# Loading the b21 slices of a seven-product block during the fifth product instead of the sixth

## The chip, the cores and the metric

The kernel runs on one core of one Trainium2 chip. The metric is the device time of one execution in microseconds (us). The kernel before takes 2382.98 us, the median of three runs (2380.82 to 2383.87).

## What is computed

The reference is a decoder trunk of two layers on 256 tokens of width 2048, in float32. Each layer normalises its input, projects it with one large matrix `w_in`, feeds two token mixers (eight heads of differential attention, sixteen heads of stick-breaking attention), gates each mixer's output, projects both, merges them by two sigmoid gates and adds one last projection to the residual:

```
h = rms_norm(x, norm_gain)
proj = h @ w_in            # da_q da_k da_v da_z sb_q sb_k sb_v sb_z gate_a gate_b, 2048 columns each
ua = rms_norm(differential_attention(...)) * (1 - lambda_init) * silu(da_z)
ub = stick_breaking_attention(...) * silu(sb_z)
y = sigmoid(gate_a) * (ua @ w_branch_a) + sigmoid(gate_b) * (ub @ w_branch_b)
x = x + y @ w_out
```

## The kernel before, in words

**Weights in slices.** Every weight matrix is cut into chunks of 512 columns, and each chunk into eight slices of 256 rows (128 partitions x 1024 float32, 512 KB). A slice is loaded into a tile `raw` by `load_raw` (line 91, the DMA is issued on SyncE's queue at line 93). There are twelve `raw` tiles (`RAW = 12`). `split_raw` (line 96) makes two tiles of it: ScalarE copies it in a rounded form into `wh` (four buffers, line 65), and VectorE writes the remainder into `wl` (three buffers, line 66). When VectorE has written `wl`, nothing reads `raw` any more, and its place is free for another load, unless the block still needs it. Each product of a slice is then three matmuls on TensorE (`mm3`, lines 70 to 72): high times high, high times low, and low times high; they read `wh`, `wh` and `wl`.

**Two kinds of streams.** `c_stream` (line 121) multiplies one chunk in the plain way: eight steps, one slice and 12 matmuls each, summed in PSUM tiles `mc`. `s_stream` (line 149) multiplies two neighbouring chunks at once with seven products instead of eight, each of four steps of one slice and six matmuls, 28 steps in all. It uses four groups of four slices: b11 and b21 (upper and lower half of the left chunk), b12 and b22 (of the right one). In the order of the program, for the variant that the change touches:

- first product, `sU`: the b11 slices are loaded into four tiles `xs`; after each step, GpSimd issues a DMA that adds b12 to `xs[i]` (line 169);
- second product, `sN`: the b22 slices are loaded into four tiles `zs`;
- third product, `sQ`, reads `xs[i]`; then VectorE adds `zs[i]` to `xs[i]` (line 173) and GpSimd issues a DMA that adds b12 to `zs[i]`;
- fourth product, into `sU` again, reads `xs[i]`;
- fifth product, `sQ` (line 235), reads `zs[i]`: each of its steps frees one `zs` tile;
- sixth product, `sN` (line 246), loads the b21 slices into four tiles `ws` and reads them; after each step VectorE adds `ws[i]` to `xs[i]` (`add_w`, line 242, by way of line 173), and `ws[i]` is free;
- seventh product, into `sQ`, reads `xs[i]` and frees it.

The names first to seventh product are used below. The flag `tb_dma` selects a variant in which the b12 and b22 additions are made by DMA and the fifth product comes before the fourth; it is on for the first three stick-breaking groups of each layer and off for the last group and for the three blocks of the merge that compute the gates (`gate_block`, line 855). So each layer has four blocks of the variant above, and the program has eight. In the merge they run beside the plain streams of `w_a` and `w_b`; they are called gate block one, two and three below.

**The order of the work.** `run` (line 256) interleaves two streams: it always takes the next step of the one that is relatively further behind. In the merge 64 units of plain streams (each chunk has eight steps and two empty ones, `GAP`) run beside 84 steps of three blocks. What `run` yields is the order of the program. From this order and from a time model a scheduler at build time derives one fixed order for each engine and for each DMA queue. The splits and the additions of line 173 are under `high_priority(offset=400)` (lines 98, 168, 172): they count as 400 places earlier in the program than they stand. The loads have no such offset. The scheduler gives a load one of the twelve `raw` places when it is free, and the load waits for the last reader of that place.

Around the fifth and sixth product of gate block two, `run` gives this order of slices (worked out from its rule; a3 l4 is the fifth slice of the last chunk of `w_a`, and "five 0" is the first step of the fifth product):

```
five 0, a3 l4, five 1, five 2, a3 l5, five 3, a3 l6, six 0 (ws0), a3 l7, six 1 (ws1), six 2 (ws2), six 3 (ws3)
```

After this come the first slices of `w_b`, and in the first chunk of `w_b` three reloads of a gated mixer output (`reload("b", ...)`, line 763, called at line 838): a `raw` tile is loaded from DRAM and split into tiles `ub`.

Of the kernel before, what the change touches and what calls it, by code (L numbers as in the profile page):

```python
# [42 lines left out]
def trunk(ctx: ExitStack, tc: tile.TileContext, x, xT, norm_gain, w_in, qk_gain, lam_vecs,  # L43
# [24 lines left out]
    def mm3(ps, lh, ll, rh, rl, start, stop, more=False):  # L68
        kw = dict(skip_group_check=True) if more else {}
        nc.tensor.matmul(ps, lhsT=lh, rhs=rh, start=start, stop=False, **kw)  # L70
        nc.tensor.matmul(ps, lhsT=lh, rhs=rl, start=False, stop=False, **kw)  # L71
        nc.tensor.matmul(ps, lhsT=ll, rhs=rh, start=False, stop=stop, **kw)  # L72
# [12 lines left out]
    def raw_tile():  # L85
        return wp.tile([P, KK * CW], F32, name="raw", bufs=RAW)

    def held(nm):
        return wp.tile([P, CW], F32, name="pp", bufs=PPB)

    def load_raw(src):
        raw = raw_tile()
        nc.sync.dma_start(out=raw, in_=src)
        return raw

    def split_raw(raw):
        h = wp.tile([P, KK * CW], F32R, name="wh", bufs=4)
        l = wp.tile([P, KK * CW], F32R, name="wl")
        with tc.high_priority(offset=400):
            split(h, l, raw)  # L100
        return h, l
# [47 lines left out]
    def s_stream(sl, sr, xh, sm, fin, tb_dma=False):  # L149

        hk = KP // 2
        b11, b21, b12, b22 = sl[:hk], sl[hk:], sr[:hk], sr[hk:]
        xs, zs, ws = [None] * hk, [None] * hk, [None] * hk

        def a(half, t):  # L160
            ts = slice(t * P, (t + 1) * P)
            return [xh[i][:, half * KT // 2:(half + 1) * KT // 2, ts] for i in range(2)]

        def s(j):
            return [sm[i][:, j] for i in range(2)]

        def add_dma(dst, src):
            with tc.high_priority(offset=400):
                nc.gpsimd.dma_start(out=dst, in_=src, accum_op=ALU.add)  # L169

        def add(dst, src):
            with tc.high_priority(offset=400):
                nc.vector.tensor_tensor(out=dst, in0=dst, in1=src, op=ALU.add)  # L173

        def prod(ps, lhs, get, after=None, more=False):
            for i in range(hk):
                raw = get(i)
                h, l = split_raw(raw)
                for kk in range(KK):
                    k = i * KK + kk  # L180
                    cs = slice(kk * CW, (kk + 1) * CW)
                    mm3(ps, lhs[0][:, k], lhs[1][:, k], h[:, cs], l[:, cs],
                        k == 0 and not more, k == KT // 2 - 1, more)
                if after is not None:
                    after(i)
                if i < hk - 1:
                    yield

        def loader(store, srcs):
            def get(i):  # L190
                store[i] = load_raw(srcs[i])
                return store[i]
            return get


        u_ps = ps_s.tile([P, CW], F32, name="sU")
        yield from prod(u_ps, a(0, 0), loader(xs, b11), lambda i: add_dma(xs[i], b12[i]))
        p1 = held("p1")
        nc.scalar.copy(p1, u_ps)
        yield  # L200

        n_ps = ps_s.tile([P, CW], F32, name="sN")
        yield from prod(n_ps, s(3), loader(zs, b22),
                        (lambda i: add_dma(zs[i], b12[i])) if tb_dma else None)
        yield


        def next_sums(i):
            if tb_dma:
                add_dma(xs[i], b22[i])  # L210
            else:
                add(xs[i], zs[i])
                add_dma(zs[i], b12[i])

        q_ps = ps_s.tile([P, CW], F32, name="sQ")
        yield from prod(q_ps, s(0), lambda i: xs[i], next_sums)
        p5 = held("p5")
        nc.scalar.copy(p5, q_ps)
        yield
        if tb_dma:  # L220
            v_ps = ps_s.tile([P, CW], F32, name="sQ")
            yield from prod(v_ps, s(2), lambda i: zs[i], None, False)
            yield

        yield from prod(u_ps, s(1), lambda i: xs[i], None, True)
        w = held("w")
        nc.vector.tensor_tensor(out=w, in0=u_ps, in1=p5, op=ALU.subtract)
        u = held("u")
        nc.scalar.copy(u, u_ps)
        fin(1, 0, lambda dst: nc.vector.tensor_tensor(out=dst, in0=n_ps, in1=w, op=ALU.subtract))  # L230
        yield

        if not tb_dma:
            v_ps = ps_s.tile([P, CW], F32, name="sQ")
            yield from prod(v_ps, s(2), lambda i: zs[i], None, False)
        fin(1, 1, lambda dst: nc.vector.scalar_tensor_tensor(
            out=dst, in0=v_ps, scalar=-1.0, in1=w, op0=ALU.mult, op1=ALU.subtract))
        if not tb_dma:
            yield


        def add_w(i):
            add(xs[i], ws[i])

        r_ps = ps_s.tile([P, CW], F32, name="sN")
        yield from prod(r_ps, a(1, 0), loader(ws, b21), add_w)
        fin(0, 0, lambda dst: nc.vector.tensor_tensor(out=dst, in0=r_ps, in1=p1, op=ALU.add))
        yield

        yield from prod(v_ps, a(1, 1), lambda i: xs[i], None, True)  # L250
        fin(0, 1, lambda dst: nc.vector.tensor_tensor(out=dst, in0=v_ps, in1=u, op=ALU.add))
        yield
# [159 lines left out]
    for l in range(DEPTH):  # L412
# [37 lines left out]
        def w_chunk(base, g):  # L450
            return [w_in[l, base + g, kp] for kp in range(KP)]
# [324 lines left out]
        for g in range(NG):  # L776
            wT = sb_weights(g)
            if g == NG - 1:
                reload("a", (0, 1), ua)
            v = v_tiles()  # L780
            gz = att.tile([P, NT, CW], F32, name="gz")
            gzT = []

            def z_T():
                gzT.append(att.tile([P, HPG, S], F32, name="gzT", tag="hold"))
                for t in range(NT):
                    tr = ps_at.tile([P, CW], F32, name="at")
                    for h in range(HPG):
                        nc.tensor.transpose(out=tr[:, h * P:(h + 1) * P],
                                            in_=gz[:, t, h * P:(h + 1) * P], identity=ident)  # L790
                    nc.scalar.copy(gzT[0][:, :, t * P:(t + 1) * P], heads(tr))

            fv, fz = vz_fin(v, gz, z_T)
            s = s_stream(w_chunk(SB_V, g), w_chunk(SB_Z, g), xt, sm,
                         lambda col, t, op: (fv, fz)[col](t, op), g + 1 < NG)
            if g + 1 < NG:
                c = [q_stream(NG + g + 1, xt, False, GAP), k_stream(NG + g + 1, xt, False, GAP)]
            else:
                c = [gate_chunk("a", 0), gate_chunk("a", 1)]
            run((len(c) * (C_STEPS + GAP), chain(*c)), (S_STEPS, s))  # L800
            last_u = sb_out(g, wT, v, gzT[0])
# [53 lines left out]
        def gate_block(b, c):  # L855
            return s_stream(w_chunk(GATE_A if b == "a" else GATE_B, c),
                            w_chunk(GATE_A if b == "a" else GATE_B, c + 1), xt, sm, sig_s_fin(b, c))
# [98 lines left out]
```

## Time and profile before

| What | Value |
|---|---|
| Median of three runs | 2382.98 us (2380.82 to 2383.87) |
| The profiled execution, its own time | 2380.12 us |
| The profiled execution, span from the first to the last instruction | 2378.4 us |
| Bytes moved | 535.55 MB, 225 GB/s over the span |

Times in the profile are counted from the span's start. PE is TensorE, DVE is VectorE, ACT is ScalarE, POOL is GpSimd, SP is SyncE; a q behind the name is the engine's queue, which issues DMAs. A row of the timeline gives start, duration, engine, line, operation, output and inputs, and in brackets the idle time of the engine before it and what ended that idle time. Instructions of the same kind that follow without a gap are merged into one row ("x2").

### The profile page before, as it was taken

To read this page: it belongs to the slowest core of one execution; us is meant where nothing else is said; L and a number is where in the kernel's file an instruction comes from. 1 tells how busy PE (TensorE), PEld (TensorE's weight loads), DVE (VectorE), ACT (ScalarE), POOL (GpSimd) and SP (SyncE) were. 2 spreads that over 40 slices of the span, in tenths; PEclk is the share of its full clock that TensorE was granted. 3 is DMA by queue.
4 is the path that set the end of the run, shared out by engine and by line. 5 is a ranking of instruction groups with operands and counts; after the bars stand their busy time and mean duration, and the time that the engine had idled before them with its cause. 6 is when DMAs were issued, how large, how long until landed. Compare 5 with 4: busy or idle time off the path is not lost.

```text
span 2378.4 us, 31466 instructions
## 1 busy us (share of the span) xinstructions
PE 2356.9 (99%) x10996; PEld 1955.5 (82%) x10996; DVE 1781.6 (75%) x2000; ACT 1529.9 (64%) x2201; POOL 341.1 (14%) x399
## 2 busy tenths in 40 slices
PE   9999999999999999999999999999999999999999
PEld 7888888888888888788888888888888888887887
DVE  6777768688788888786566777676887887878854
ACT  7666666677777666554465666666767776656643
POOL 1231220201101011100020312202011010111000
PEclk9999999999999999999999999999999999999999
DMA  9546546878877888898665465468789778988972
GB/s 367 179 143 210 196 142 221 198 224 235 238 234 209 266 274 247 293 287 271 207 211 177 142 213 187 141 226 209 224 233 241 234 210 254 289 237 285 298 264 89
DMA packets 152239, 535.55 MB, mean 225 GB/s; under 512 B 17360, under 2 KB 17872, under 8 KB 152080
## 3 DMA queue, kind: packets, MB, share of 16 engines
q1 hardware_dynamic: 123552, 432.72, 53.3%
q0 software_dynamic: 28096, 100.42, 19.9%
q8 instruction: 86, 1.41, 0.2%
q14 instruction: 73, 0.60, 0.1%
q10 hardware_dynamic: 432, 0.40, 0.1%
HBM read 509.35 MB, written 24.12 MB: 224 GB/s over the span
## 4 chain that ended last, share of the span: by engine, by line
PE 96%; DMA 2%; DVE 1%; ACT 1%; issue 0%; DVEq 0%; SPq 0%; ACTq 0%
PE mc L71 16%; PE mc L72 16%; PE mc L70 16%; PE sU L71 6%; PE sU L72 5%; PE sU L70 5%; PE sN L71 5%; PE sN L72 5%; PE sN L70 5%; PE sQ L71 3%; PE sQ L70 3%; PE sQ L72 3%; PE at L277 2%; PE at L71 1%; PE at L72 1%; PE at L70 1%
## 5 line engine op out<-in xcount | busy, mean ns | idle before, releaser
L66 DVE TENSOR_TENSOR wl<-raw,wh 128x1024 fp32r<-128x1024 f32 (+1 forms) x1001 | 1212.5, 1222 | 391.9 <-PE mc L71 155.9
L65 ACT CAST wh<-raw 128x1024 fp32r<-128x1024 f32 (+1 forms) x1001 | 1047.5, 1051 | 642.2 <-PE mc L72 340.7
L169 POOL DMA_DIRECT2D raw<-in_w_in x136 | 117.8, 867 | 835.4 <-DVE wl L66 429.3
L71 PE MATMUL mc<-wl,xTh 128*128 128x512 f32 x576 | 225.1, 391 | 2.5 <-DVE wl L66 2.4
L72 PE MATMUL mc<-wh,xTl 128*128 128x512 f32 x576 | 224.4, 390 | 0.0
L70 PE MATMUL mc<-wh,xTh 128*128 128x512 f32 x576 | 206.8, 391 | 0.0
L70 PE MATMUL mc<-wh,xrh 128*128 128x512 f32 x512 | 197.6, 393 | 5.7 <-ACT wh L65 5.7
L71 PE MATMUL mc<-wl,xrh 128*128 128x512 f32 x512 | 200.5, 392 | 0.0
L72 PE MATMUL mc<-wh,xrl 128*128 128x512 f32 x512 | 200.3, 392 | 0.0
L71 PEld LDWEIGHTS mc<-wl,xTh 128*128 128x128 f32 x576 | 108.1, 188 | 26.2 <-DVE wl L66 4.2
L70 PEld LDWEIGHTS mc<-wh,xTh 128*128 128x128 f32 x576 | 107.7, 188 | 22.7 <-ACT wh L65 0.6
L72 PEld LDWEIGHTS mc<-wh,xTl 128*128 128x128 f32 x576 | 108.2, 188 | 21.9
L70 PEld LDWEIGHTS mc<-wh,xrh 128*128 128x128 f32 x512 | 96.6, 189 | 25.5 <-ACT wh L65 5.7
L173 DVE TENSOR_TENSOR raw<-raw 128x1024 f32<-128x1024 f32 x88 | 107.2, 1221 | 13.3 <-DMA raw<-in_w_in 12.2
L71 PEld LDWEIGHTS mc<-wl,xrh 128*128 128x128 f32 x512 | 96.6, 189 | 19.5 <-DVE wl L66 0.2
L72 PEld LDWEIGHTS mc<-wh,xrl 128*128 128x128 f32 x512 | 96.5, 188 | 19.3
L71 PE MATMUL sU<-wl,xrh 128*128 128x512 f32 x256 | 100.7, 393 | 0.1
L72 PE MATMUL sN<-wh,xrl 128*128 128x512 f32 x256 | 100.3, 392 | 0.0
L70 PE MATMUL sN<-wh,xrh 128*128 128x512 f32 x256 | 100.1, 391 | 0.0
L71 PE MATMUL mc<-wl,ua 128*128 128x512 f32 x256 | 100.0, 390 | 0.0
L71 PE MATMUL sN<-wl,xrh 128*128 128x512 f32 x256 | 100.0, 390 | 0.0
L70 PE MATMUL sU<-wh,xrh 128*128 128x512 f32 x256 | 100.0, 390 | 0.0
(254 smaller groups left out, 4913.6 us busy)
## 6 DMA issues: line engine op xcount, KB each, us to landing
raw<-in_w_in SPq DMA_DIRECT2D x583, 512.0 KB, 4.4
raw<-in_w_in POOLq DMA_DIRECT2D x136, 512.0 KB, 7.6
raw<-in_w_a SPq DMA_DIRECT2D x64, 512.0 KB, 5.3
raw<-in_w_b SPq DMA_DIRECT2D x64, 512.0 KB, 5.8
raw<-in_w_o SPq DMA_DIRECT2D x64, 512.0 KB, 4.5
ua<-us POOLq DMA_DIRECT2D x8, 512.0 KB, 5.9
raw<-ua SPq DMA_DIRECT2D x8, 512.0 KB, 4.8
siga<-tok POOLq DMA_DIRECT2D x16, 256.0 KB, 5.3
```

The costliest lines, as they stand in the source:

```text
L65: nc.scalar.copy(h, src)
L66: nc.vector.tensor_tensor(out=l, in0=src, in1=h.bitcast(F32), op=ALU.subtract)
L70: nc.tensor.matmul(ps, lhsT=lh, rhs=rh, start=start, stop=False, **kw)
L71: nc.tensor.matmul(ps, lhsT=lh, rhs=rl, start=False, stop=False, **kw)
L72: nc.tensor.matmul(ps, lhsT=ll, rhs=rh, start=False, stop=stop, **kw)
L169: nc.gpsimd.dma_start(out=dst, in_=src, accum_op=ALU.add)
L173: nc.vector.tensor_tensor(out=dst, in0=dst, in1=src, op=ALU.add)
L277: nc.tensor.transpose(out=tr[:, j * P:(j + 1) * P], in_=src[:, j * P:(j + 1) * P], identity=ident)
```

## The change: what it does

In the variant without `tb_dma`, each step of the fifth product now also issues the load of one b21 slice, after its own matmuls. The sixth product takes the tiles that are there already. The variant with `tb_dma` does what it did before: there `ws[i]` is still empty, and the slice is loaded in the sixth product. No instruction is added or taken away; 32 loads (four in each of eight blocks) stand at another place in the program.

```diff
+        def early(i):
+            ws[i] = load_raw(b21[i])
+
         if not tb_dma:
             v_ps = ps_s.tile([P, CW], F32, name="sQ")
-            yield from prod(v_ps, s(2), lambda i: zs[i], None, False)
+            yield from prod(v_ps, s(2), lambda i: zs[i], early, False)
...
         r_ps = ps_s.tile([P, CW], F32, name="sN")
-        yield from prod(r_ps, a(1, 0), loader(ws, b21), add_w)
+        yield from prod(r_ps, a(1, 0), lambda i: ws[i] if ws[i] is not None else loader(ws, b21)(i),
+                        add_w)
```

With the rule of `run`, the order of slices around the same place of gate block two becomes:

```
five 0 (ws0), a3 l4, five 1 (ws1), five 2 (ws2), a3 l5, five 3 (ws3), a3 l6, six 0, a3 l7, six 1, six 2, six 3
```

## The prediction

> **What bounds the kernel now.** I read the page first, then the busy times by stage, then the list of waits, and then the timelines of the queue and of the engines around the fifth, sixth and seventh product.
>
> ```profile
> span 2378.4 us, 31466 instructions
> PE 2356.9 (99%) x10996; PEld 1955.5 (82%) x10996; DVE 1781.6 (75%) x2000; ACT 1529.9 (64%) x2201; POOL 341.1 (14%) x399
> L65 ACT CAST wh<-raw 128x1024 fp32r<-128x1024 f32 (+1 forms) x1001 | 1047.5, 1051 | 642.2 <-PE mc L72 340.7
> ```
>
> TensorE is busy in all but 21.5 us of the span, and the change takes no matmul away. So only idle time of TensorE can be won, and only where the moved loads have an influence. I asked for the busy times of the eight stretches that begin with the fifth product of a block of the variant without `tb_dma` and end with its seventh. In these rows the columns are the stretch, its length, and the busy time of PE, PEld, DVE, ACT and POOL with the number of instructions, then the granted clock, the busy share of the DMA engines and GB/s; the last row sums all eight.
>
> ```profile
> 940.40:982.00 41.60, 38.41 (x167) 30.90 (x166) 34.99 (x34) 25.18 (x28) 4.74 (x8) 1.00 0.93 325
> 1032.00:1069.10 37.10, 36.72 (x162) 29.72 (x161) 30.58 (x31) 21.73 (x23) 1.68 (x3) 1.00 0.92 318
> ...
> 2125.00:2166.00 41.00, 39.66 (x169) 31.11 (x168) 35.87 (x35) 25.87 (x28) 3.66 (x6) 1.00 0.91 313
> ...
> sum 300.30, PE 295.39 PEld 241.22 DVE 251.64 ACT 189.62 POOL 22.10; mean PE 36.92 PEld 30.15 DVE 31.45 ACT 23.70 POOL 2.76
> ```
>
> The eight stretches hold 300.30 - 295.39 = 4.9 us of idle TensorE. All of it lies in the three stretches shown: 3.2 us and 1.3 us in gate block two of the first and of the second layer, 0.4 us in gate block three of the first. In the other five TensorE never idles. That is all that this change can win if nothing elsewhere moves. For comparison, 0.2% of the kernel, about what a measurement of it can tell from no change, is 4.8 us.
>
> **When the moved loads run now.** The next rows are the queue of SyncE and its waits (in all, times, longest).
>
> ```profile
> SPq L93 <- DVE wl L66: 1812.5, 699, 25.1
> ```
>
> ```profile
> 926.28 8.74 SPq L93 DMA_DIRECT2D raw<-in_w_a  x3
> 937.64 0.33 SPq L93 DMA_DIRECT2D raw<-in_w_in  x1
> 939.90 0.33 SPq L93 DMA_DIRECT2D raw<-in_w_a  x1
> 941.26 0.33 SPq L93 DMA_DIRECT2D raw<-in_w_in  x1
> 941.64 0.90 SPq L815 DMA_DIRECT2D tok<-siga  x2
> 944.73 3.46 SPq L93 DMA_DIRECT2D raw<-in_w_in  x2
> ```
>
> The queue has 699 waits for VectorE to finish reading a `raw` tile: a load goes out when a place is free, not when the program reaches it. The order of issues is that of the program: a3 l4, l5, l6 (the row with x3), ws0, a3 l7, ws1, then ws2 and ws3 (944.73 and, 3.46 - 0.33 later, 947.86). So the b21 slices are already loaded during the fourth and the fifth product; the first matmul of the fifth product comes at about 940.4, where the stretch begins. The words of the change describe the program, not the chip.
>
> From this follows how I treat the edit. Places come free at the same moments as before, since TensorE's pace frees them; the change only permutes which load takes which moment. The eight moments above now go to ws0, a3 l4, ws1, ws2, a3 l5, ws3, a3 l6, a3 l7.
>
> **Part one: the b21 slices come earlier.** ws0 moves from 937.64 to 926.28, ws1 from 941.26 to about 934.7 (the row x3 ends at 926.28 + 8.74 = 935.02, and its last issue took 0.33), ws2 from 944.73 to 937.64, ws3 from 947.86 to 941.26: 6.6 to 11.4 us earlier. Who waits for them today is `add_w` on VectorE. I show this in gate block two of the second layer, by the rows of VectorE, SyncE's queue, ScalarE and TensorE.
>
> ```profile
> DVE raw L173 <- DMA raw<-in_w_in: 12.2, 13, 2.0
> ```
>
> ```profile
> 2135.51 1.22 DVE L173 TENSOR_TENSOR raw<-raw 128x1024 f32<-128x1024 f32 x1 [1.58 <-DMA raw<-in_w_in]
> 2136.66 2.35 DVE L66 TENSOR_TENSOR wl<-raw,wh 128x1024 fp32r<-128x1024 f32 x2
> ```
>
> ```profile
> 2137.90 0.33 SPq L93 DMA_DIRECT2D raw<-ub  x1
> ```
>
> ```profile
> 2142.79 1.05 ACT L65 CAST ub<-raw 128x1024 fp32r<-128x1024 f32 x1 [4.34 <-DMA raw<-ub]
> ```
>
> ```profile
> 2146.29 0.50 PE L71 MATMUL sN<-wl,xTh 128*128 128x512 f32 x1 [0.36 <-DVE wl L66]
> ...
> 2150.63 0.50 PE L71 MATMUL sN<-wl,xTh 128*128 128x512 f32 x1 [0.59 <-DVE wl L66]
> ```
>
> VectorE works in order. It stands 1.58 us for a b21 slice, the two `wl` behind the addition are late, the first of them frees its place only at about 2137.9, the reload of `ub` goes out then, ScalarE stands 4.34 us for it, and with ScalarE late VectorE falls behind until TensorE waits. With the slice there 6 us earlier this wait and the additions (1.22 us each) move into the fourth product, and the reload goes out up to 1.58 + 1.22 = 2.8 us sooner. I take the 1.3 us of this stretch as won. The 0.4 us of gate block three I also take as won, by likeness: a wait of the same kind is among the 13.
>
> In gate block two of the first layer the idle time has two pieces:
>
> ```profile
> 964.57 0.50 PE L71 MATMUL sN<-wl,xTh 128*128 128x512 f32 x1 [0.77 <-DVE wl L66]
> ...
> 976.71 0.50 PE L71 MATMUL sQ<-wl,xTh 128*128 128x512 f32 x1 [2.41 <-DVE wl L66]
> ```
>
> ```profile
> 973.21 1.05 ACT L65 CAST ub<-raw 128x1024 fp32r<-128x1024 f32 x1 [4.39 <-DMA raw<-ub]
> ```
>
> ```profile
> GB/s 242 109 156 359 343 359 351 312 187 320 359 226 226 281 257 281 265 265 312 328 296 257 273 257 320 375 398 437 429 406 421 429 414 406 414 414 398 429 421 437
> ...
> raw<-ub SPq DMA_DIRECT2D x2, 512.0 KB, 7.8
> ```
>
> The first (0.77) is the same backlog, and I take it as won. The second (2.41) hangs on the third reload of `ub`, which lands at 973.2. The last two rows are the transfers of 954 to 975, the rate in 40 slices and the median from issue to landing. Near the end of that stretch the engines move 400 to 437 GB/s, and a load issued a little sooner only queues sooner: I leave the 2.41 us where they are. The Trainium skill ("DMA: Bandwidth & Descriptors", section Bandwidth) puts the ceiling of a core's DMA engines at about 435 GB/s; the last slice, at 437, agrees. By that rule the sum stays as I have it; were the load free to move with its place, the piece would go too and the sum would be 4.9.
>
> Sum of part one: 1.3 + 0.4 + 0.8 = 2.5 us won.
>
> **Part two: the plain stream's slices come later.** a3 l5, l6 and l7 now go out at 939.90, 944.73 and 947.86. When they are needed stands in TensorE's rows: each plain slice opens with a pair of matmuls of line 70, and these are the last three pairs of this chunk, those of l5, l6 and l7.
>
> ```profile
> 948.37 0.61 PE L70 MATMUL mc<-wh,ua 128*128 128x512 f32 x2
> ...
> 952.45 0.61 PE L70 MATMUL mc<-wh,ua 128*128 128x512 f32 x2
> ...
> 956.53 0.61 PE L70 MATMUL mc<-wh,ua 128*128 128x512 f32 x2
> ```
>
> ```profile
> raw<-in_w_a SPq DMA_DIRECT2D x4, 512.0 KB, 4.4
> ```
>
> From issue to first use l5 keeps 8.5 us, l6 7.7 and l7 8.7 (l6 had up to 17.8 before). A landing of 4.4 us, the median from 926 to 951, and the copy to `wh` of 1.05 us need 5.5. So the tightest keeps 2.2 us. Its cost is nothing as long as a landing takes less than 7.7 - 1.05 = 6.65 us; beyond that TensorE stands for the difference.
>
> The tightest place is gate block three, where loads are slower:
>
> ```profile
> raw<-in_w_b SPq DMA_DIRECT2D x5, 512.0 KB, 6.9
> ```
>
> This is the median from 1016 to 1040. With the same 7.7 us it leaves 7.7 - 6.9 - 1.05 = -0.2 us: two such blocks, 0.5 us at most. Since part one empties VectorE's queue at the same place I count this as nothing and keep it for the range.
>
> **Part three: the additions stand elsewhere.** The four additions (4 x 1.22 us) of each block move toward the fourth product. Queued behind each on VectorE are the `wl` of the next slices, for which TensorE waits. In the fourth product of gate block one VectorE is busy 10.68 of 13 us:
>
> ```profile
> 845.00:858.00 13.00, 13.00 (x59) 10.77 (x58) 10.68 (x11) 8.24 (x9) 0.58 (x1) 1.00 0.86 250
> ```
>
> That leaves 2.3 us, so two additions fit there and two stay in the fifth product, from which they came. An addition costs TensorE at most its own 1.22 us where it falls into a dense place, and below nothing it cannot be, as its work is the same. I take nothing, and keep 2 x 1.22 = 2.4 us for the range.
>
> The sum is -2.5 us. Against the profiled execution (2380.12 us, its span of 2378.4 and 1.7 us around it) that is 2377.6; the median of the runs is 2.9 us above that execution, so I forecast 2382.98 - 2.5 = **2380.5 us**.
>
> **The rivals.**
>
> *The additions still chase their loads.* The scheduler puts a prioritised addition where it believes its load has landed, so 13 waits may simply move along with the loads. For it: the loads still go out when a place is free. Against it: the dense stretch of reloads comes after, and would be spared anyway. Then the idle time stays: 2383.0. The Trainium skill ("Trainium Kernel Development and Optimization", Key Constraints) says that DMAs of all queues run on the same 16 engines; the busy shares of 0.91 to 0.93 in the three stretches agree, and speak for this rival.
>
> *Everything goes.* If the third reload does move with its place, all 4.9 us are won: 2378.1.
>
> *The plain stream starves.* Slower: the three late slices have 7.7 us instead of up to 17.8. If landings in these windows take 8.3 us, 1.4 more than the 6.9 measured in gate block three, the tightest slice of each of the six gate blocks is 8.3 + 1.05 - 7.7 = 1.65 us late, together 9.9 us: 2392.9. It begins at 6.65 us. For it: 6.9 stands in a row, and the loads after 954 take 7.8. Against it: the bytes go out at the same moments as before, so the landings should not change.
>
> *It does nothing*, since the loads were early already, falls together with the first rival.
>
> **How the numbers follow.** The forecast gets 0.45, the first rival 0.19, everything goes 0.20, starving 0.16. Faster by over 0.2% means below 2378.2: over half of the third case, and a little of the forecast's, since the order fixed at build time may shift other stalls too; 0.16 in all. How much that can be, the three stretches tell: the same gate block two idles 3.2 us in one layer and 1.3 us in the other, 1.9 us apart. Slower by over 0.2% means above 2387.7: nearly all of the last case, 0.15. The rest, 0.69, lies within. The range goes from 2376.5 (all 4.9 us, and 1.6 us for such a shift) to 2387.5 (no gain, the 2.4 us of part three, the 0.5 us of part two, and 1.6 us); outside it lie most of the starving case and a small remainder below.
>
> **What would show it.** Right: loads of b21 in the queue's rows one to three slices ahead of where they were; no wait of line 173 for a DMA just before the reloads; in gate block two of the second layer the reload goes out 1.5 to 2.8 us sooner relative to its block, and TensorE does not idle there. The 2.41 us before the last `sQ` of the first layer's gate block two remain. Wrong: TensorE idles "<-ACT wh" or "<-DVE wl" at the opening of plain slices during the fifth and sixth product (starving), or the list of line 173's waits has the same sum of about 12 us with the idle time unchanged (chasing), or TensorE's idle time changes in stages that hold none of the eight blocks.

## The result and the profile after

| Kernel | Median | Range | Runs |
|---|---|---|---|
| before | 2381.93 us | 2378.51 to 2383.87 | 6 |
| after | 2392.51 us | 2390.62 to 2395.21 | 6 |

The changed kernel is slower: ratio 1.0049, 95% interval 1.0038 to 1.0060. The forecast was 2380.5 us with a range up to 2387.5; the result lies 5 us above its end. The profiled execution of the kernel after is the slowest of its six, 2395.21 us, 15.1 us above that of the kernel before, while the medians lie 10.6 us apart.

The page of the kernel after:

```profile
span 2393.4 us, 31477 instructions
...
PE 2362.8 (99%) x10996; PEld 1956.7 (82%) x10996; DVE 1781.6 (74%) x2000; ACT 1529.9 (64%) x2201; POOL 341.2 (14%) x399
```

The work is the same: as many instructions on each engine, VectorE busy for the same 1781.6 us. The span has grown by 15.0 us, TensorE's busy time by 5.9, so 9.1 us are new idle time.

Where it lies, by stretches. Each row is one block from its first product to the next block: the stretch, its length, and the busy time of PE, PEld, DVE, ACT and POOL, then the granted clock, DMA share and GB/s. The three rows are gate blocks two and three of the first layer and gate block three of the second; the sum is over all eight blocks that the change touches. First the kernel before:

```profile
891.50:982.00 90.50, 87.31 (x383) 71.42 (x382) 72.91 (x67) 54.44 (x57) 13.32 (x19) 1.00 0.91 279
982.00:1069.00 87.00, 86.62 (x386) 71.01 (x386) 70.03 (x65) 50.98 (x53) 8.26 (x11) 1.00 0.88 272
...
2165.80:2252.10 86.30, 86.30 (x386) 71.11 (x385) 69.97 (x66) 51.02 (x53) 8.26 (x11) 1.00 0.88 273
sum 711.70, PE 703.93 PEld 579.65 DVE 589.39 ACT 456.62 POOL 81.60; mean PE 87.99 PEld 72.46 DVE 73.67 ACT 57.08 POOL 10.20
```

Then the kernel after:

```profile
893.20:989.00 95.80, 89.72 (x384) 72.47 (x383) 73.10 (x67) 54.55 (x57) 13.39 (x19) 0.98 0.87 274
989.00:1078.60 89.60, 87.56 (x386) 70.76 (x385) 69.81 (x66) 50.52 (x53) 8.26 (x11) 1.00 0.83 253
...
2177.20:2267.10 89.90, 87.07 (x386) 70.94 (x385) 69.82 (x66) 50.55 (x53) 8.26 (x11) 1.00 0.84 259
sum 725.80, PE 709.06 PEld 579.83 DVE 589.40 ACT 456.54 POOL 81.60; mean PE 88.63 PEld 72.48 DVE 73.68 ACT 57.07 POOL 10.20
```

The eight blocks are 725.80 - 711.70 = 14.1 us longer, nearly all of the 15.0. They lose 16.74 us of TensorE's time to idling instead of 7.77. Gate block two of the first layer alone grows by 5.3 us, gate block three by 2.6 and 3.6; that of the second layer, where TensorE never idled, now idles 2.8 us.

What the engines wait for, from the lists of waits (in all, times, longest). VectorE in the kernel after, against 12.2 us, 13 times, 2.0 before:

```profile
DVE raw L173 <- DMA raw<-in_w_in: 28.5, 20, 3.5
```

TensorE in the kernel after:

```profile
PE mc L71 <- DVE wl L66: 8.1, 10, 1.5
...
PE sQ L70 <- ACT wh L65: 5.5, 4, 3.8
```

The same two rows in the kernel before:

```profile
PE mc L71 <- DVE wl L66: 2.4, 3, 1.0
...
PE sQ L70 <- ACT wh L65: 0.2, 1, 0.2
```

The waits of `add_w` did not vanish, they more than doubled. How they reach TensorE is seen in gate block three of the first layer of the kernel after. First SyncE's queue: these are the issues of the first, the second and the last of the four b21 slices.

```profile
1022.67 0.33 SPq L93 DMA_DIRECT2D raw<-in_w_in  x1
...
1032.29 0.33 SPq L93 DMA_DIRECT2D raw<-in_w_in  x1
...
1043.11 0.33 SPq L93 DMA_DIRECT2D raw<-in_w_in  x1
```

Then VectorE, in brackets how long it stood before the row:

```profile
1029.90 1.23 DVE L173 TENSOR_TENSOR raw<-raw 128x1024 f32<-128x1024 f32 x1 [2.71 <-DMA raw<-in_w_in]
1031.04 3.49 DVE L66 TENSOR_TENSOR wl<-raw,wh 128x1024 fp32r<-128x1024 f32 x3
1035.60 1.22 DVE L173 TENSOR_TENSOR raw<-raw 128x1024 f32<-128x1024 f32 x1 [1.07 <-DMA raw<-in_w_in]
...
1044.06 1.23 DVE L173 TENSOR_TENSOR raw<-raw 128x1024 f32<-128x1024 f32 x1 [1.37 <-DMA raw<-in_w_in]
...
1051.41 1.23 DVE L173 TENSOR_TENSOR raw<-raw 128x1024 f32<-128x1024 f32 x1 [2.71 <-DMA raw<-in_w_in]
1052.56 2.35 DVE L66 TENSOR_TENSOR wl<-raw,wh 128x1024 fp32r<-128x1024 f32 x2
```

And TensorE:

```profile
1032.31 0.50 PE L71 MATMUL mc<-wl,ub 128*128 128x512 f32 x1 [0.72 <-DVE wl L66]
...
1053.83 0.50 PE L71 MATMUL sQ<-wl,smh 128*128 128x512 f32 x1 [0.70 <-DVE wl L66]
```

The slice goes out at 1022.67, VectorE reaches its addition at 1029.90 - 2.71 = 1027.2 and stands until 1029.9. The `wl` of a `w_b` slice is queued behind the addition, begins at 1031.04, and TensorE goes on at 1032.31, after 0.72 us without work. The same happens at 1051.41, before the pause of 0.70 us that ends at 1053.83. In all four cases VectorE comes to the addition 2.2 to 5.6 us after the issue of the load, and the load lands 3.3 to 8.3 us after it (1035.60 - 1032.29 for the second slice, 1051.41 - 1043.11 for the last).

The largest single loss is in gate block two of the first layer, where the third reload of `ub` now holds up TensorE for longer. ScalarE, and then TensorE:

```profile
977.47 1.04 ACT L65 CAST ub<-raw 128x1024 fp32r<-128x1024 f32 x1 [6.49 <-DMA raw<-ub]
```

```profile
979.51 0.50 PE L70 MATMUL sQ<-wh,xTh 128*128 128x512 f32 x1 [3.81 <-ACT wh L65]
```

Before it was 4.39 us for ScalarE and 2.41 for TensorE. And the pause has an after-effect. In the stretches behind it the column after POOL is the granted clock:

```profile
975.00:979.50 4.50, 0.71 (x4) 0.24 (x2) 0.95 (x1) 2.03 (x3) 0.00 (x0) 1.00 1.03 422
979.50:982.00 2.50, 2.49 (x9) 2.03 (x10) 2.44 (x3) 2.38 (x3) 0.54 (x1) 0.80 1.02 410
982.00:985.00 3.00, 3.00 (x10) 2.34 (x9) 1.51 (x3) 1.04 (x1) 0.00 (x0) 0.60 1.02 408
```

The clock fell to 0.80 and 0.60: 0.2 x 2.5 + 0.4 x 3.0 = 1.7 us of TensorE's speed lost while the page of the profile counts it busy. That is part of the 5.9 us by which busy time grew. The rest was not traced to single rows.

### The profile page after: what moved, and what is told of

It reads as the page before. It is cut to its first block, busy times and chain, and to the rows that moved or that the text cites. A ratio compares the mean times of both kernels' runs of the same rounds, so it can differ in the third digit from the quotient of the medians.

```text
span 2393.4 us, 31477 instructions
## 1 busy us (share of the span) xinstructions
PE 2362.8 (99%) x10996; PEld 1956.7 (82%) x10996; DVE 1781.6 (74%) x2000; ACT 1529.9 (64%) x2201; POOL 341.2 (14%) x399
## 4 chain that ended last, share of the span: by engine, by line
PE 94%; DMA 2%; DVE 2%; ACT 1%; issue 1%; SPq 0%; DVEq 0%; ACTq 0%
PE mc L71 16%; PE mc L72 16%; PE mc L70 16%; PE sU L71 5%; PE sU L70 5%; PE sU L72 5%; PE sN L71 5%; PE sN L72 5%; PE sN L70 5%; PE sQ L70 3%; PE sQ L71 3%; PE sQ L72 3%; PE at L281 2%; DVE wl L66 2%; DMA raw<-in_w_in 1%; PE at L71 1%
## 5 line engine op out<-in xcount | busy, mean ns | idle before, releaser
L173 DVE TENSOR_TENSOR raw<-raw 128x1024 f32<-128x1024 f32 x88 | 107.3, 1222 | 29.3 <-DMA raw<-in_w_in 28.5
```

## The experiments

Theory A: the additions of b21 stand in VectorE's fixed order where the scheduler believes the load to have landed; they move along with the loads, VectorE stands for the loads, and the splits queued behind come late to TensorE. Theory B: the slices of the plain streams, which gave up their turns in the queue, come late.

| Kernel | Median us | Ratio to before (95%) |
|---|---|---|
| after, addition without a load to wait for | 2378.07 | 0.9991 (0.9981 to 1.0000) |
| before, the same | 2375.01 | 0.9975 (0.9966 to 0.9985) |
| after, addition without priority | 2393.58 | 1.0052 (1.0040 to 1.0065) |
| before, the same | 2380.04 | 1.0002 (0.9993 to 1.0011) |
| before, addition behind its split, everywhere | 2395.14 | 1.0063 (1.0050 to 1.0076) |
| after, the same | 2393.17 | 1.0056 (1.0043 to 1.0068) |
| after, loads two steps ahead | 2389.05 | 1.0044 (1.0031 to 1.0058) |
| after, no load to wait for, plain slices ahead | 2377.20 | 0.9986 (0.9977 to 0.9995) |
| after, addition on GpSimd | 2398.59 | 1.0078 (1.0066 to 1.0091) |
| before, the same | 2395.26 | 1.0059 (1.0046 to 1.0071) |
| after, addition behind its split, eight blocks | 2384.26 | 1.0018 (1.0010 to 1.0027) |
| before, the same | 2384.18 | 1.0018 (1.0009 to 1.0027) |
| after, addition by DMA | 2422.90 | 1.0184 (1.0170 to 1.0198) |
| before, the same | 2385.93 | 1.0025 (1.0015 to 1.0034) |
| before, plain slices ahead | 2385.35 | 1.0025 (1.0016 to 1.0034) |
| after, the same | 2390.19 | 1.0044 (1.0031 to 1.0056) |
| after, addition one step early | 2383.32 | 1.0014 (1.0005 to 1.0023) |
| after, addition two steps early | 2378.97 | 0.9996 (0.9988 to 1.0005) |

Each was timed beside the kernel before on the same chip, whose median in the five sets was 2380.59, 2380.89, 2379.71, 2379.80 and 2379.85 us.

**Nothing to wait for.** In both kernels the addition adds the tile `xs[i]` to itself, so that it needs no load; b21 is left out of the seventh product's input. The work of VectorE stays, and so does the order of the loads. But the additions do not stay where they were: with no load to follow, the scheduler puts them earlier. In gate block two of the first layer of the kernel before, the first two moved from 941.75 and 945.47 to 931.29 and 935.83, into the fourth product, which ends at 941.4 there. One row of this run, and one of the kernel before:

```profile
935.83 2.36 DVE L173 TENSOR_TENSOR raw<-raw 128x1024 f32<-128x1024 f32 x2
```

```profile
945.47 1.22 DVE L173 TENSOR_TENSOR raw<-raw 128x1024 f32<-128x1024 f32 x1 [0.77 <-DMA raw<-in_w_in]
```

So the pair takes away the wait and changes the place at once.

```diff
         def add_w(i):
-            add(xs[i], ws[i])
+            add(xs[i], xs[i])
```

> The kernel after, but the addition that follows the sixth product adds xs[i] to itself instead of ws[i]; the b21 slices are therefore left out of the seventh product's input. Same work on VectorE, same loads at the same places, but the addition no longer waits for a load. Theory A (VectorE stands in order for a b21 slice and the wl behind it come late): the loss of 10.6 us goes, 2380 to 2384 us. Theory B (the plain stream's slices come late because the b21 slices hold places, the starving rival of the prediction): the loss stays, 2390 to 2394. Both at work: 2385 to 2389.

> Control: the same edit in the kernel before (xs[i] is added to itself, b21 is left out of the seventh product's input), where 13 waits with 12.2 us in all go. Theory A: a little faster than before, up to the 2 us of TensorE's idle time that hang on these waits, 2379 to 2382. Theory B: no change, 2381 to 2383.

Measured: 2378.07 and 2375.01, both below the range that theory A gave. With no load to wait for, the 10.6 us between the two kernels shrink to 3.1. In the kernel before, the waits and the places of the additions together cost 2380.59 - 2375.01 = 5.6 us. The additions of the two runs stand alike (931.57 and 936.11 in the kernel after), so the 3.1 us that stay come from the order of the loads. They speak for theory B, and ScalarE's waits for plain slices do appear. The kernel after with the self-addition, and below it the kernel before:

```profile
ACT wh L65 <- DMA raw<-in_w_a: 11.6, 9, 3.0
```

```profile
ACT wh L65 <- DMA raw<-in_w_a: 0.4, 2, 0.2
```

**No priority.** The addition loses its offset of 400 places.

```diff
         def add_w(i):
-            add(xs[i], ws[i])
+            nc.vector.tensor_tensor(out=xs[i], in0=xs[i], in1=ws[i], op=ALU.add)
```

> The kernel after with the addition of ws[i] kept, but without its priority of 400 places, so that the scheduler puts it after the splits of its neighbourhood. Theory A: VectorE's waits for b21 slices (28.5 us in the kernel after) fall below 5 us and the loss goes, 2380 to 2385. Theory B: 2390 to 2394.

> Control: the same edit in the kernel before. Theory A: the 12.2 us of waits go, 2379 to 2382; if the late addition instead holds up the seventh product, slower, 2383 to 2390. Theory B: no change, 2381 to 2383.

Measured: 2393.58 and 2380.04, both as without the edit. In the kernel after the waits hardly changed:

```profile
DVE raw L246 <- DMA raw<-in_w_in: 26.6, 17, 3.4
```

So it is not the priority that puts the additions early. The fall in waits that theory A expected here did not come in either kernel (in the kernel before 10.5 us stay of 12.2), so this pair does not tell the theories apart; the scheduler puts an addition early with or without its offset.

**A fixed place behind the split.** Each addition is fixed on VectorE directly behind the split of the same slice in the sixth product. That split reads the slice too, so the addition cannot be the one that stands for the load. First everywhere, and later only in the eight blocks:

```diff
         def add_w(i):
-            add(xs[i], ws[i])
+            if tb_dma:
+                add(xs[i], ws[i])
+            else:
+                tc.keep_in_program_order(nc.vector.tensor_tensor(out=xs[i], in0=xs[i], in1=ws[i], op=ALU.add))
```

> The kernel before, with each addition of a b21 slice fixed on VectorE directly behind the split of that same slice in the sixth product. The split reads the slice, so the addition can no longer be the instruction that stands for the load. Theory A (the additions stand in order for their loads, and the splits queued behind them come late to TensorE): the waits of the addition for a DMA fall from 12.2 us to under 1 us, and the time comes close to the 2375.0 of the kernel before without that wait: 2374.5 to 2377.5. Rival (what costs is not the wait but the place: four additions of 1.22 us between the splits of the sixth product, where VectorE is dense): the waits go too, but the time stays at 2380 or rises above.

> The kernel after, with the same fixed place of the additions. Theory A: the waits of the addition for a DMA fall from 28.5 us to under 1 us and most of the 12 us of loss go. Theory B (the slices of the plain streams come late, since the b21 slices took their turns in the queue) leaves its share: 3 us above the kernel before with the same edit, so 2378 to 2380.5, with 8 to 12 us of waits of ScalarE for slices of w_a. Rival (there is no share B, the 3.1 us between the two kernels without the wait came from another order): the same time as the kernel before with this edit, within 1 us.

> The kernel after with each addition fixed behind the split of its own slice, in the eight changed blocks alone. The earlier run fixed the additions of the six other groups as well, and its stretches show about 2 us lost in each of those, some 11 us in all. Theory A: 2393.2 less these 11 is 2382 to 2384, so that the 12 us of loss are undone apart from what the dense place of the additions costs. Rival (it is the changed blocks that lose in that run): 2390 or more.

> The kernel before with the additions fixed behind the split in the eight blocks alone. By the same reckoning 2395.1 less 12 is 2382 to 2384: without any wait of an addition, the early place that the additions have in the kernel before is worth about as much as their waits cost. Compared with the kernel after under the same edit it shows what the order of the loads does by itself once no addition can stand for a load: theory B says that the kernel after is 2 to 3 us slower, the rival that the two are the same within 1.5 us.

Fixed everywhere, both kernels are slow (2395.14 and 2393.17). Both expectations were missed: the edit also moved the additions of the six `tb_dma` groups, and those cost 2395.14 - 2384.18 = 11 us (9 us in the kernel after). In the eight blocks alone the result is clear: 2384.26 and 2384.18, 0.2 to 0.3 us above what was expected. With the additions at a fixed late place the two orders of the loads take the same time, although the plain slices still come late in the kernel after:

```profile
ACT wh L65 <- DMA raw<-in_w_a: 12.5, 9, 2.8
```

The list of the kernel before has no such row. So late plain slices alone cost nothing that can be measured; theory B fails here. The late place itself costs 4 us in both, though no addition waits for a load in either. A likely reason is that VectorE is dense there (before the edit it is busy 4.94 of the 5 us from 960 to 965, in the sixth product); it was not tried by itself.

**Half the dose.** The kernel after, with each b21 slice loaded two steps ahead of its own step.

```diff
         def early(i):
-            ws[i] = load_raw(b21[i])
+            if i >= 2:
+                ws[i - 2] = load_raw(b21[i - 2])
...
+        def add_and_load(i):
+            add_w(i)
+            if not tb_dma and i < 2:
+                ws[i + 2] = load_raw(b21[i + 2])
```

> Half the dose: in the program each b21 slice is loaded two steps before its own step of the sixth product (two of them in the fifth product, two in the sixth) instead of four or more. Theories A and B both see a smaller permutation: waits of the addition for a DMA between 12.2 and 28.5 us, say 18 to 22, waits of ScalarE for w_a about 4 us, and a time between the two kernels, 2385 to 2389. Rival (a threshold: only the loads in the first two steps of the fifth product meet the rush of other loads): the time of the kernel before, within 2 us.

Measured: 2389.05, between the two kernels, at the upper end of the expected range, with 25.9 us of waits of the addition, more than expected. The rival, which puts it at the time of the kernel before, fails. And ScalarE's list has no wait for `w_a` here, where both theories expected 4 us: so 8 us of loss (1.0044) stand with no late slice of `w_a`.

**Plain slices ahead.** The plain streams of `w_a` and `w_b` load two of their steps ahead, so that they get back about the turns that the b21 slices took.

```diff
         for i, kp in enumerate(depth):
...
-                h, l = split_raw(load_raw(src[kp]))
+                while len(raws) < min(i + 1 + ahead, KP):
+                    raws.append(load_raw(src[depth[len(raws)]]))
+                h, l = split_raw(raws[i])
```

> The kernel after without the addition's wait (each addition adds the tile to itself, so that b21 is left out of the seventh product's input), and besides that the plain streams of w_a and w_b load their slices two of their steps ahead, so that they get back about the turns in the queue that the b21 slices took. Theory B: the waits of ScalarE for slices of w_a fall from 11.6 us to under 4, and of the 3.1 us between 2378.1 (after without the wait) and 2375.0 (before without the wait) at least 2 us go: 2374.5 to 2376.5. Rival (the order of the loads is not the cause, or loading further ahead only delays others in turn): 2378 or above, with the waits merely at another place.

> The kernel before with the slices of w_a and w_b loaded two of their steps ahead in the program, the additions as they are. Theory A: the b21 slices now come later still against the plain ones and the additions are placed behind them; their waits stay near 12 us. In the run of the kernel after with the self-addition gate block two lost its idle time with this edit, the third reload of ub among it; if that holds here, 3 to 5 us go: 2376 to 2379. Rival (what is loaded ahead only takes the turns of others): 2380 to 2384, with waits at other loads.

> The kernel after with the slices of w_a and w_b loaded two of their steps ahead, the additions as they are. If late plain slices carry most of the loss, the time falls from 2392.5 to 2384 or less. If the standing of the additions carries it (theory A), their waits of 28.5 us stay within 5 us and the time stays at 2387 to 2392.

Measured: 2377.20, 2385.35 and 2390.19. Beside the self-addition the edit won 0.9 of the 3.1 us, less than theory B asked for and too little to tell from nothing. ScalarE's waits for `w_a` went altogether, but those for `in_w_in` rose from 21.6 to 29.3 us, as the rival had it. The kernel before lost 5.5 us by the edit, against the expected gain and more than the rival had; why was not traced. The kernel after stayed where it was (1.0044 against 1.0049), and so did the additions' waits, as theory A had it:

```profile
DVE raw L176 <- DMA raw<-in_w_in: 25.1, 19, 3.6
```

**On GpSimd.** The additions of the eight blocks are made by GpSimd.

```diff
-            add(xs[i], ws[i])
+            with tc.high_priority(offset=400):
+                (nc.vector if tb_dma else nc.gpsimd).tensor_tensor(out=xs[i], in0=xs[i], in1=ws[i], op=ALU.add)
```

> The kernel after, with the additions of b21 in the eight blocks that the change touches made by GpSimd instead of VectorE; the computation is the same. GpSimd may stand for the load, and no split is queued behind it. From its rows of 128x256 elements (0.92 to 1.70 us) an addition of 128x1024 should take 3.7 to 6.8 us, four of them up to 27 us, beginning in the fifth product. Theory A (in-order standing of VectorE is what costs): most of the 12 us go, what stays is the share of the late plain slices, 3 us over the kernel before with the same edit; 2378 to 2383. Rival (the early loads themselves cost, through the DMA engines or the reloads of ub): 2388 or more although no addition stands on VectorE.

> The kernel before with the same move of the additions to GpSimd in the eight blocks. Theory A: the 5.6 us that the waits cost go, 2374 to 2377, and VectorE is relieved of 32 additions of 1.22 us besides. Rival (GpSimd's additions are so slow that the splits of the seventh product, which read the sums, come late): above 2383, with TensorE idle for splits at the opening of the seventh product.

Measured: 2398.59 and 2395.26, both slower, and not for a reason that either expectation names. GpSimd in the kernel before with this edit, then VectorE beside it:

```profile
949.32 3.07 POOL L244 TENSOR_TENSOR raw<-raw 128x1024 f32<-128x1024 f32 x1 [3.33 <-DMA raw<-in_w_in]
953.60 6.61 POOL L244 TENSOR_TENSOR raw<-raw 128x1024 f32<-128x1024 f32 x2 [1.21 <-DVE wl L66]
```

```profile
950.20 3.26 DVE L66 TENSOR_TENSOR wl<-raw,wh 128x1024 fp32r<-128x1024 f32 x1
```

```profile
954.53 6.76 DVE L66 TENSOR_TENSOR wl<-raw,wh 128x1024 fp32r<-128x1024 f32 x2
```

These additions take 3.1 to 3.3 us, and a split that begins during one takes 3.3 to 3.4 us instead of 1.22. The first one ends 953.46 - 952.39 = 1.07 us after the addition, so it did nothing until GpSimd had finished. The Trainium skill ("SBUF — State Buffer", Who interferes with whom) says that VectorE and GpSimd share one pair of ports, which one of them holds alone; the trace agrees, with that 1.07. VectorE was still held up, now inside its splits by GpSimd instead of by the load, so this pair tells nothing of theory A.

**By DMA.** In the eight blocks b21 is added to `xs[i]` by an accumulating DMA, which reads it from DRAM once more.

```diff
-            add(xs[i], ws[i])
+            add(xs[i], ws[i]) if tb_dma else add_dma(xs[i], b21[i])
```

> The kernel after, with b21 added to the xs tiles in the eight blocks by an accumulating DMA from DRAM (512 KB each, 32 in all) instead of by VectorE; the computation stays whole. No addition stands on VectorE, and none is queued on GpSimd but the issue of the DMA. Theory A: at least 8 of the 12 us go, 2378 to 2384; the plain slices still come late, by theory B up to 3 us. Rival (the early loads cost by themselves): 2390 or more. A cost on the way could be the 16.8 MB of added traffic, where the DMA engines are over 90% busy: later reloads of ub, some us.

> The kernel before with b21 added by the accumulating DMA in the eight blocks. Theory A: the waits of 12.2 us and 32 additions of 1.22 us leave VectorE, 2374 to 2378, unless the added 16.8 MB delay the reloads of ub. Rival (the added traffic costs more than the waits): above 2382, with longer waits of ScalarE for raw<-ub than 15.0 us. The difference between this run and the kernel after with the same edit is what the order of the loads does with VectorE free of additions: by theory B about 3 us, by the runs with fixed additions about 0.

Measured: 2422.90 and 2385.93. The kernel before is 6 us slower, on the side of the rival that the added traffic costs more than the waits (ScalarE's waits for the reloads of `ub` are 15.8 us, against 15.0). In the kernel after the plain streams starve; its lists of waits of ScalarE and of TensorE:

```profile
ACT wh L65 <- DMA raw<-in_w_a: 47.0, 13, 7.1
```

```profile
PE mc L70 <- ACT wh L65: 33.5, 11, 4.8
```

From issue to landing in gate block one of the first layer (840 to 885):

```profile
raw<-in_w_a SPq DMA_DIRECT2D x8, 512.0 KB, 6.5
raw<-in_w_in POOLq DMA_DIRECT2D x7, 512.0 KB, 10.1
raw<-in_w_in SPq DMA_DIRECT2D x6, 512.0 KB, 8.5
```

So the slices that gave up their turns do have too little room, once landings take 6.5 to 10 us. The change alone does not lengthen the landings that far: the same three medians are 4.6, 7.2 and 5.8 us in the kernel after.

**The loads of the kernel after, the additions where there is room.** The loads stay in the fifth product. Each addition is fixed one or two steps (`k`) earlier than behind its own split, the first ones behind the last splits of the fifth product. (In each of the two runs `k` is written as its number.)

```diff
+        def add_w(i):
+            if tb_dma:
+                add(xs[i], ws[i])
+            elif 0 <= i + k < hk:
+                j = i + k
+                tc.keep_in_program_order(nc.vector.tensor_tensor(out=xs[j], in0=xs[j], in1=ws[j], op=ALU.add))
+
         def early(i):
             ws[i] = load_raw(b21[i])
+            add_w(i - hk)
...
-        def add_w(i):
-            add(xs[i], ws[i])
```

> The loads of the kernel after, and in the eight blocks each addition of a b21 slice fixed on VectorE one step of the sixth product earlier than in the run that fixed it behind the split of its own slice (the first one behind the last split of the fifth product). The loads stand four steps ahead, so the additions should find them landed. Theory A (all of the loss lies in where the additions stand): waits of the additions under 3 us, and a time between the 2384.3 of the later place and the 2375 to 2378 without a wait: 2378 to 2382. Rival (the early loads cost by themselves): 2384 or more.

> The same with the additions fixed two steps early (the first two behind the last two splits of the fifth product). They are nearer to where the kernel before has them, VectorE has more room there, and the loads are two steps ahead. Theory A: waits of the additions up to 8 us, if the loads land late, and 2376 to 2381: the gain that was forecast for the change. Rival (the early loads cost by themselves, or each place costs alike): 2384 or more.

Measured: 2383.32, above the range that theory A gave, and 2378.97, within it. Two steps early the kernel takes the time of the kernel before (0.9996), where the changed kernel stood at 1.0049: 0.53% or 12.6 us for the place of 32 additions, with the early loads in the same order. First its queue in gate block two of the first layer, then VectorE:

```profile
925.96 0.33 SPq L93 DMA_DIRECT2D raw<-in_w_in  x1
```

```profile
945.09 1.22 DVE L238 TENSOR_TENSOR raw<-raw 128x1024 f32<-128x1024 f32 x1
```

The first addition comes 19.1 us after the load's issue and waits for nothing; the list of waits has no row of an addition for a DMA. What keeps the time from falling to 2375 was not tried. TensorE has a wait that the kernel before with the self-addition has not:

```profile
PE sQ L70 <- ACT wh L65: 5.4, 5, 1.9
```

And ScalarE's list has rows that are longer than there (5.9 and 0.4 us):

```profile
ACT ub L65 <- DMA raw<-ub: 12.6, 6, 5.9
...
ACT wh L65 <- DMA raw<-in_w_a: 8.4, 6, 3.0
```

So the reloads of `ub` and some slices of `w_a` still come late. No version with the whole computation beat the kernel before by more than the 0.2% that can be told.

## Why the prediction was wrong

**The inventory of idle time was right.** 4.9 us was to be won at most. With nothing to wait for, the kernel before gained 5.6 us, and in its trace the eight blocks have none of that idle time left: TensorE idles 2372.4 - 2355.7 = 16.7 us in all, against 21.5.

**The order of the queue was right.** "Places come free at the same moments as before; the change only permutes which load takes which moment": in gate block two of the first layer of the kernel after the issues went ws0, a3 l4, ws1, ws2, a3 l5, ws3, a3 l6, a3 l7, as predicted. Counted from the start of the block, which comes 1.7 us later, the seven moments that the prediction names came 0 to 2.6 us after their forecast.

**Part one failed, and the prediction with it.** "With the slice there 6 us earlier this wait and the additions (1.22 us each) move into the fourth product": from this the 1.3, 0.4 and 0.8 us were taken as won, as if the wait, once moved, were gone. The additions did move: in gate block two of the first layer the first two now start at 934.22 and 941.85, in the fourth product, which ends at 942.4. But their slices had not landed when VectorE came to them, and it stood 0.54 and 1.86 us for them. The wait came along and grew, from 12.2 to 28.5 us in all, and the splits behind it came late to TensorE (8.1 instead of 2.4 us at the plain streams), so the -2.5 us never came. That the scheduler's time model believes the loads to land sooner than they do is inferred from these rows; no run shows the model itself. The runs show the step: with the additions fixed two steps early and the loads in their new order the loss is gone (0.9996), and with the additions fixed at the late place the two orders of the loads lie 0.1 us apart, with intervals of 2 us.

**The rival that named the mechanism was mispriced.** "The additions still chase their loads" assumed that the same 13 waits move along and cost the same: 2383.0. There were 20, the longest 3.5 us instead of 2.0. Why they grew was not tried by itself. Slower landings may have a part in it: the median of the four b21 loads between 926 and 951 was 5.0 us, against 3.8 before.

**The 2.41 us piece** did not stay. The reload of `ub` goes out later (966.70 instead of 962.80), the pause grew to 3.81 us, and the fall of the clock added 1.7. Nor did the piece hang on the landing alone, as the prediction had it: in the kernel before with the self-addition the reload lands at 972.40 instead of 973.21, only 0.8 us sooner, and TensorE has no pause there at all. Before it stood for the reload, VectorE had done two splits there (from 968.78) instead of one (from 969.03), which may be why; it was not tried.

**Part two** was counted at nothing below a landing of 6.65 us. The plain slices do come late for ScalarE, 8 to 13 us in all, and between the two orders of loads lie 0.1 us with the additions at a fixed late place and 3.1 us with nothing to wait for. Why these two differ stays open. Of the 3.1 only 1.2 us are idle time of TensorE (16.7 and 17.9 us in the two traces); the rest stands in the traces as busy time. "The plain stream starves" had nearly the right time, 2392.9, by luck: its mechanism carries at most those 3 us here. It came true in the kernel after with the addition by DMA.

**Part three** counted the additions at nothing, at most 2.4 us for their own work. The work is the same (VectorE is busy 1781.6 us in both kernels); what they cost is the standing in front of the splits, and that was the term of the sum that was missing. Nor is the work a bound where VectorE has no room: at the late place, with no wait at all, the additions cost 4 us.

## What to carry over

A load that is moved can take with it whatever a build-time scheduler orders by its expected landing. Ask where the readers of the tile will stand in their engine's order afterwards, and what is queued behind them there, before counting a wait as won. A reader that is not urgent is fixed behind work that is surely later than the load, at a place where its engine has room; moving it to another engine is no way out when that engine blocks the first.

## What the runs showed of the hardware

**The clock after a pause.** In the kernel after, a pause of TensorE of 3.81 us was followed by 5.5 us at a granted clock of 0.80 and 0.60. The kernel after with the addition by DMA shows it after shorter ones; first TensorE's rows, then the stretches behind them:

```profile
868.49 0.73 PE L70 MATMUL mc<-wh,ua 128*128 128x512 f32 x2 [2.73 <-ACT wh L65]
```

```profile
1058.78 0.73 PE L70 MATMUL mc<-wh,ub 128*128 128x512 f32 x2 [2.29 <-ACT wh L65]
```

```profile
869.50:873.00 3.50, 3.50 (x10) 2.71 (x10) 1.42 (x2) 0.88 (x1) 0.58 (x1) 0.53 1.00 353
```

```profile
1060.00:1066.00 6.00, 6.00 (x20) 4.83 (x20) 5.62 (x7) 3.28 (x4) 0.00 (x0) 0.72 1.03 410
```

The 2.41 us pause of the kernel before, which ends at 976.71, had no such effect:

```profile
975.00:979.50 4.50, 2.79 (x12) 2.33 (x13) 4.50 (x5) 3.67 (x4) 0.54 (x1) 1.00 1.02 411
```

So each of these three pauses cost 1.6 to 1.7 us on top (0.47 x 3.5, 0.28 x 6.0 and the 1.7 above), and the length of a pause alone does not decide. In the kernel after with the addition by DMA a pause of 2.13 us, which ends at 2265.56, was followed by a clock of 0.50 for 2.5 us, and one of 1.97 us, which ends at 2072.26, by 1.00. The Trainium skill ("TensorE: Matmul & The Clock Gate", What's actually happening) puts the array at half clock after an idle window of about 3.4 us. The 3.81 us agree; the shorter pauses do not, though their lengths go by modelled ends of matmuls.

**GpSimd beside VectorE.** In the kernel before with this edit the 32 additions of 128x1024 on GpSimd took 2.4 to 3.5 us (median 3.1) against 1.22 on VectorE. The ones shown above stopped a VectorE split for as long as they ran; one that began with no split running beside it, at 942.94, took 2.4 us.
